# Merge gates moved to the front as seven half-size products a pair, and one fixed order of TensorE for the band, the linear attention and the second branch

## The chip, the cores and the metric

The kernel runs on one core of one Trainium2 chip. The metric is the device time of one launch in microseconds (us). Five engines work side by side: TensorE (PE, with its weight loads as PEld), VectorE (DVE), ScalarE (ACT), GpSimd (POOL) and SyncE (SP, which issues most DMAs). Each works through its own queue of instructions, and semaphores order the queues among one another.

## What is computed

One layer of a streaming encoder for 1056 tokens, 1024 of a prompt and 32 of a second request. In the reference, cut to what matters here:

```python
h = rms(x); z = h @ w_in   # -> GLA q,k,v,r,gate rank | band q,k,v | merge gates gA,gB
# branch A: gated linear recurrence, 4 heads
b = cumsum(log_a); scores = einsum(q_i, k_j, exp(b_i - b_j))   # causal
o = scores @ v + (q * exp(b)) @ S;  S = exp(b_last) * S + (k * exp(b_last - b))^T @ v
A = (rms(o) * g_gla * silu(r)) @ w_br_a
# branch B: softmax attention over a band of 64-frame chunks, 8 heads
B = band_attend(q, k, v, rel_bias) @ w_br_b
mix = (sigmoid(gA) * A + sigmoid(gB) * B) @ w_out;  x += rms(mix)
# then a ConvFFN and a per-layer embedding, which the change does not touch
```

The model width is 1024; gA and gB are 1024 columns each.

## The kernel before

Activations are kept transposed: features on the 128 partitions, the 1056 tokens along the free axis, in eight tiles of 128 features and three spans of 352 tokens (`CHUNKS`). A large product in fp32 accuracy is made of three matmuls for each block of 128x128 weights: high part of the weights by high part of the activations, high by low, low by high (`product`, L221 to L227). `weights` (L191) loads 512 KB of raw weights by a DMA on SP's queue, ACT rounds off the high part (`whi`, L204), POOL subtracts to get the low part (`wlo`, L205). `project` (L445) makes one tile of 128 columns of `w_in`: 8 blocks by 3 matmuls for each of 3 spans, 72 matmuls of 352 columns, and DVE takes each span out of PSUM with the factor 1/rms (L457).

The stages: a prologue (per-layer embedding product, split of x into `xh` and `xl`, the squares and the gate rank, L303 to L404), the band attention (four pairs of heads: scores, L541 and L542, DVE maximum L548, ACT exponential L550, transposes L557, product with v L599), the linear attention GLA (four heads), the second branch (band output times `w_br_b`, L987 to L1002), then branch A's product, `w_out`, the ConvFFN and the embedding. The merge gates (L634 to L642) are 16 calls of `project`, each with a sigmoid and a store to DRAM. They are emitted in portions after the pairs of the band and the heads of GLA (`BAND_GATES`, `GLA_GATES`), to be worked on between the attention's own steps.

A GLA head works in four segments of 256 tokens (the last has 288). For each, DVE and ACT build the decayed rows: differences `d` (L823), exponentials on ACT, products into the tile `x` (L826, L831), of which there are two buffers. PE makes scores from `x`, a diagonal (L851) and six levels (L859); DVE copies them into `scores` under masks (`copy_predicated`, L871, L875, L907); PE transposes one half of `scores` (L895) and multiplies by v and by the state (L917, L919). Once for each head stands the decay: three products by `wa` (L797), DVE L799, ACT exponential and logarithm, and DVE scans (L804).

The prologue and all that follows the second branch have their order written out by hand. The stages between are ordered by a scheduler when the kernel is built, from priorities and data dependences, engine by engine. What comes out is a fixed row of instructions for each engine, and each is worked through in that order.

## Time and profile before

| what | value |
|---|---|
| three runs | 1907.05, 1910.38, 1910.48 us; median 1910.38 |
| the profiled execution: span | 1907.2 us, 3.2 us under the median of the runs |
| TensorE busy | 1883.0 us in 13364 records |
| VectorE busy | 1263.1 us in 2533 |
| ScalarE busy | 908.4 us in 1674 |
| GpSimd busy | 464.8 us in 568 |
| prologue, band, GLA, second branch, rest | 0 to 44, 44 to 387, 387 to 880, 880 to 922, 922 to 1907 us |

A line of groups reads: line, engine, operation, output and inputs by the program's names, shape, count, then busy time and the mean duration in ns of one, then the time for which the engine stood idle ahead of them with what ended it. A line of windows reads: the stretch, its length, then for PE, PEld, DVE, ACT and POOL the busy us with the number of instructions, the granted clock of TensorE, the DMA share and GB/s. A busy TensorE says that its queue was never empty, not that each matmul had the shortest spacing; the spacing is the length of a window divided by its matmuls.

### The profile page before, as it was taken

Reading aid. Unit: us, or ns where it says so; the run is one execution under the profiler, and the core shown is the slowest. Engines: PE = TensorE matmul, PEld = TensorE weight load, DVE = VectorE, ACT = ScalarE, POOL = GpSimd, SP = SyncE. Lnnn points to the kernel's source line nnn. Section 1 sums busy time; section 2 is a strip of 40 time slices with the busy share of each in tenths; the row PEclk is TensorE's granted clock in tenths of the full one; section 3 lists DMA queues with packets and bytes.
Section 4 is the critical chain, followed back from the end, with each engine's and each line's share of the span. In section 5 each row is a group of like instructions: output and inputs, shape, how many; then the busy total and the mean of one; then the engine's idle time right before and its main releaser. Section 6 shows DMA issues by size and latency. Waiting matters only on the chain.

```text
span 1907.2 us, 34216 instructions
## 1 busy us (share of the span) xinstructions
PE 1883.0 (99%) x13364; PEld 1853.8 (97%) x13364; DVE 1263.1 (66%) x2533; ACT 908.4 (48%) x1674; POOL 464.8 (24%) x568
## 2 busy tenths in 40 slices
PE   9999999999999999999999999999999999999997
PEld 8999999999999999999999999999999999999997
DVE  6656556448487385675564787887777776556886
ACT  7456465434373352764334554434334344445554
POOL 2322222232222121221220113332222222115312
PEclk9999999999999999999999999999999999999999
DMA  7324346435344322227885356543433448556677
GB/s 275 121 98 131 109 126 166 108 123 152 100 139 128 110 73 80 92 92 265 313 281 184 108 171 224 188 168 124 158 128 128 144 150 298 190 187 195 216 262 148
DMA packets 107053, 307.77 MB, mean 161 GB/s; under 512 B 13252, under 2 KB 35724, under 8 KB 106764
## 3 DMA queue, kind: packets, MB, share of 16 engines
q1 hardware_dynamic: 80764, 217.64, 34.4%
q0 software_dynamic: 25296, 87.04, 15.5%
q8 instruction: 105, 1.72, 0.4%
q10 hardware_dynamic: 832, 0.90, 0.1%
q14 instruction: 56, 0.46, 0.1%
HBM read 217.79 MB, written 107.60 MB: 171 GB/s over the span
## 4 chain that ended last, share of the span: by engine, by line
PE 82%; DVE 10%; ACT 4%; issue 3%; DMA 1%; POOL 0%; SPq 0%; ACTq 0%; DVEq 0%; POOLq 0%
PE mm L225 13%; PE mm L226 13%; PE mm L227 13%; PE c L1748 11%; PE two L1484 6%; PE two L1486 6%; PE two L1485 6%; PE aux L1748 2%; PE one L599 2%; PE one L557 2%; PE two L859 1%; PE two L541 1%; PE one L917 1%; PE two L542 1%; DVE z L1854 1%
## 5 line engine op out<-in xcount | busy, mean ns | idle before, releaser
L225 PE MATMUL mm<-xh,whi 128*128 128x352 f32 (+2 forms) x1248 | 411.8, 330 | 0.0
L227 PE MATMUL mm<-xh,wlo 128*128 128x352 f32 (+2 forms) x1248 | 410.0, 329 | 0.0
L226 PE MATMUL mm<-xl,whi 128*128 128x352 f32 (+2 forms) x1248 | 408.6, 327 | 0.0
L205 POOL TENSOR_TENSOR wlo<-raw,whi 128x512 fp32r<-128x512 f32 x128 | 187.2, 1466 | 663.4 <-ACT whi L204 648.7
L225 PEld LDWEIGHTS mm<-xh,whi 128*128 128x128 f32 x1248 | 235.2, 188 | 2.1 <-DVE ev L457 0.7
L226 PEld LDWEIGHTS mm<-xl,whi 128*128 128x128 f32 x1248 | 235.0, 188 | 1.6 <-issue 0.7
L227 PEld LDWEIGHTS mm<-xh,wlo 128*128 128x128 f32 x1248 | 234.4, 188 | 0.9
L1486 PE MATMUL two<-mh,wlo 128*128 128x264 f32 x576 | 162.9, 284 | 0.0
L1485 PE MATMUL two<-ml,whi 128*128 128x264 f32 x576 | 162.5, 283 | 0.0
L1484 PE MATMUL two<-mh,whi 128*128 128x264 f32 x576 | 161.4, 284 | 0.4 <-ACT whi L230 0.4
L204 ACT ACTIVATE whi<-raw 128x512 fp32r<-128x512 f32 x136 | 84.1, 626 | 113.8 <-PE mm L226 84.1
L1748 PE MATMUL c<-mh,whi 128*128 128x264 f32 x396 | 112.4, 284 | 0.0
L1748 PE MATMUL c<-mh,wlo 128*128 128x264 f32 x396 | 112.3, 284 | 0.0
L1748 PE MATMUL c<-ml,whi 128*128 128x264 f32 x396 | 112.2, 283 | 0.0
L1485 PEld LDWEIGHTS two<-ml,whi 128*128 128x128 f32 x576 | 108.3, 188 | 0.0
L1486 PEld LDWEIGHTS two<-mh,wlo 128*128 128x128 f32 x576 | 108.3, 188 | 0.0
L1484 PEld LDWEIGHTS two<-mh,whi 128*128 128x128 f32 x576 | 107.3, 188 | 0.9 <-ACT whi L230 0.6
L457 DVE TENSOR_TENSOR ev<-mm,rstd 128x352 f32<-128x352 f32 x120 | 61.7, 518 | 60.4 <-PE mm L227 59.9
L1474 ACT ACTIVATE whi<-ws 128x512 fp32r<-128x512 f32 x72 | 45.5, 631 | 98.2 <-PE two L1485 63.6
L561 DVE TENSOR_TENSOR pt<-one,pt 128x128 fp32r<-128x128 f32 (+3 forms) x96 | 46.4, 499 | 51.4 <-ACT pt L560 51.2
L225 PE MATMUL mm<-mh,ahi 128*128 128x352 f32 x240 | 77.4, 322 | 0.0
L226 PE MATMUL mm<-ml,ahi 128*128 128x352 f32 x240 | 77.4, 322 | 0.0
(584 smaller groups left out, 5444.9 us busy)
## 6 DMA issues: line engine op xcount, KB each, us to landing
raw<-in_w_in SPq DMA_DIRECT2D x52, 512.0 KB, 3.8
uraw<-d_b POOLq DMA_DIRECT2D x33, 528.0 KB, 5.0
raw<-in_w_up SPq DMA_DIRECT2D x26, 512.0 KB, 3.6
d_b<-av POOLq DMA_DIRECT2D x44, 264.0 KB, 2.7
d_s<-in_w_down POOLq DMA_DIRECT2D x16, 704.0 KB, 8.3
draw<-d_s SPq DMA_DIRECT2D x16, 704.0 KB, 4.2
hn<-d_b POOLq DMA_DIRECT2D x40, 264.0 KB, 3.5
d_b<-hn POOLq DMA_DIRECT2D x40, 264.0 KB, 2.4
```

The lines of the kernel that those rows point to most:

```text
L204: ac.activation(hi[-1][:, d], raw[:, b], AF.Copy)
L205: eng.tensor_tensor(lo[-1][:, d], raw[:, b], hi[-1][:, d], op=ALU.subtract)
L225: pe.matmul(ps, h, xh(kt), start=(first and i == 0), stop=False)
L226: pe.matmul(ps, h, xl(kt), start=False, stop=False)
L227: pe.matmul(ps, l, xh(kt), start=False, stop=(last and i == n - 1))
L457: return lambda ps, s: ve.tensor_tensor(t[:, s], ps, rstd(s), op=ALU.mult)
L561: ve.tensor_tensor(out[1], tv, out[0], op=ALU.subtract)
L1474: ac.activation(h, x, AF.Copy)
L1484: pe.matmul(ps[:, j, :HC], w[0][:, k], x[0][:, k, s], start=st, stop=False, skip_group_check=True)
L1485: pe.matmul(ps[:, j, :HC], w[0][:, k], x[1][:, k, s], start=False, stop=False, skip_group_check=True)
L1486: pe.matmul(ps[:, j, :HC], w[1][:, k], x[0][:, k, s], start=False, stop=sp_, skip_group_check=True)
L1748: pe.matmul(ps, w, x, start=st, stop=sp_, skip_group_check=True)
```

## The change

It has four parts.

1. **Gates.** The 16 gate tiles are made in 8 pairs by a scheme of seven products in place of eight (`in_pair`, L566): the two column tiles, the two halves of the 1024 features and the two halves of the tokens form a 2x2 block product, DVE adds up sums of weights (`plus`, L573) and of activations (`t_scale` to `t_fourth`, L486 to L516), and each product (`mul`, L590) is 2 parts of 264 columns by 4 blocks by 3 matmuls, 24 matmuls. ACT rounds the high parts of the weights here and DVE makes the low parts (`weight`, L583). Sums of products are collected by DVE, POOL multiplies by 1/rms (`end`, L641), ACT does the sigmoid. All this stands between the prologue and the band, behind the three projections of the band's first pair.
2. **Prologue.** The sum over features for the first span (`x_total(0)`, L375) now follows the first of the three gate-rank products; it followed the third. The squares go to tiles of their own, since x is used again.
3. **Fixed order of TensorE** in band, GLA and second branch: `project` is a generator that gives three matmuls a step, and `fill(n)` puts n such steps between the steps of the attention, by the tables `BAND_FILL` and `GLA_FILL`. The projections of the next pair or head are the filling; in the last head's segments it is the second branch. DVE, ACT and POOL stay with the scheduler. The masked copies now all have high priority, and their emission precedes the rows of the following segment (`mid`, L1440), the decay of the next head (in each head's second segment) and its neighbours' factors (`gla_near`, in the third).
4. **Small ones.** The product with silu(r) leaves DVE in GLA (L947) for `row_load` in the second branch (L1374, POOL for tiles 0 to 5); q and k of head 0 are projected in the last pair of the band; in band and GLA the PSUM buffers of products (`mm`) go from three to two, those of the small matmuls (`one`) from three to four.

The core of the diff:

```diff
-PS_BAND = (3, 3, 1)
+PS_HEAD = (3, 3, 1)
+PS_BAND = (2, 4, 1)
+PS_GLA = (2, 4, 1)
+BAND_FILL = ((3, 2), (3, 2), (3, 2), (2, 1))
+GLA_FILL = ((7, 6, 6, 6), (8, 8, 8, 7), (8, 8, 8, 7), (6, 6, 6, 6))
...
     alr_product(0)
+    x_total(0)
     alr_out(0)
     alr_product(1)
+    x_inverse(0)
...
-            product(ps, hi, lo, [(k, k) for k in range(KT)], lambda k: xh[:, k, s], lambda k: xl[:, k, s])
+            for k in range(KT):
+                product(ps, hi, lo, [(k, k)], lambda k: xh[:, k, s], lambda k: xl[:, k, s], k == 0, k == KT - 1)
+                if k < KT - 1:
+                    yield
...
+        def mul(b, n, first, last):
+            if b not in ps:
+                ps[b] = bank()
+            x = XS[n]
+            for j in range(2):
+                s = slice(j * HC, (j + 1) * HC)
+                o = ps[b][0][:, j, :HC]
+                for k in range(HK):
+                    st_, sp_ = first and k == 0, last and k == HK - 1
+                    pe.matmul(o, w[n][0][:, k], x[0][:, k, s], start=st_, stop=False, skip_group_check=True)
+                    pe.matmul(o, w[n][0][:, k], x[1][:, k, s], start=False, stop=False, skip_group_check=True)
+                    pe.matmul(o, w[n][1][:, k], x[0][:, k, s], start=False, stop=sp_, skip_group_check=True)
...
+    repsum((0, 0, 4))
+    for i in range(7 * len(pairs_)):
+        if unit(i + LOOK):
+            unit(i + LOOK)[0]()
+        unit(i)[1]()
...
-    def gates(cnt):
-        for n, w0, dst in todo_gates[:cnt]:
-            g = evt()
-            project(w0 + n, to_tile(g))
-            ac.activation(g, g, AF.Sigmoid)
...
+            with tc.high_priority():
+                ve.copy_predicated(apart(pair, m), halves(masks[:, l], m), halves(place(l), m))
...
+        mid()
+        fill(F[0])
+        if before:
+            before()
+        kp = ps_one()
...
+        fill(F[1])
+        pe.transpose(kp[:, 256:384], pair[:, :P], ident)
...
+            def mid():
+                if i == 0 and h < 3:
+                    gla_load(h + 1)
+                if h == 0 and i in (0, 2):
+                    band_norm(2 + i // 2)
+                if i < 3:
+                    gla_rows(h, *SEGS[i + 1])
+                elif h < 3:
+                    gla_rows(h + 1, *SEGS[0])
+                if i == 1 and h < 3:
+                    gla_decay(h + 1)
+                if i == 2 and h < 3:
+                    while ("k", h + 1) not in ready:
+                        fill(1)
+                    gla_near(h + 1)
...
+        e.tensor_tensor(sr, l, sr, op=ALU.mult)
```

Three places of the order, as the built programs have it. First TensorE in the prologue. `accx` is the sum of squares, `was` the gate rank's weights, `mm` an accumulator in PSUM. Before, the third gate-rank product ends, and the total of the squares and the first projection follow:

```order
L384 MATMUL mm_467<-xh_133,was_154 48x352
L385 MATMUL mm_467<-xl_134,was_154 48x352
L250 MATMUL one_493<-accx_135,onesM_71 128x352
L225 MATMUL mm_573<-xh_133,whi_565 128x352
L226 MATMUL mm_573<-xl_134,whi_565 128x352
```

Of the changed kernel the same engine, where the first gate-rank product ends:

```order
L425 MATMUL mm_457<-xh_93,was_141 48x352
L426 MATMUL mm_457<-xl_94,was_141 48x352
L375 MATMUL one_474<-accx_145,onesM_71 128x352
L425 MATMUL mm_478<-xh_93,was_141 48x352
L426 MATMUL mm_478<-xl_94,was_141 48x352
```

The total (L250, now L375) has moved ahead of the second and third gate-rank products, 32 matmuls, which now queue behind it.

Second, TensorE in the second segment of GLA's head 0. Before, around its diagonals (L851) and levels (L859); `whi_5463`, `wlo_5468` and their like are weights of projections that the scheduler put between, `one_4770` is the norm of the segment ahead:

```order
L227 MATMUL mm_5497<-xh_133,wlo_5468 128x352
L225 MATMUL mm_5497<-xh_133,whi_5467 128x352
L246 MATMUL one_4770<-y_877_4771,onesHr_77 128x256
L851 MATMUL one_4837<-q_4053,k_4054 128x192 x2
L873 MATMUL one_4854<-ident_79,x_4789 128x128 x2
L859 MATMUL two_4956<-x_4906 128x128 x5
L247 MATMUL one_4770<-y_878_4772,onesHr_77 128x256
L859 MATMUL two_4956<-x_4906 128x128
L226 MATMUL mm_5497<-xl_134,whi_5467 128x352
```

Of the changed kernel, the same segment; L1239 and L1245 are the diagonals and levels, L1174 the decay products of head 1:

```order
L231 MATMUL mm_6860<-xh_93,whi_6852 128x352
L232 MATMUL mm_6860<-xl_94,whi_6852 128x352
L233 MATMUL mm_6860<-xh_93,wlo_6853 128x352
L1239 MATMUL one_6864<-q_6353,k_6354 128x192 x2
L1245 MATMUL two_6868<-x_6681 128x128 x6
L1174 MATMUL one_6934<-ev_6670,wa_1076_6672 128x352
L1174 MATMUL one_6938<-ev_6670,wa_1076_6672 128x352
L1174 MATMUL one_6942<-ev_6670,wa_1076_6672 128x352
```

Before, the levels that stand beside the second segment's diagonals are those of the third (`two_4956`); the second's own were made a segment earlier. Now each segment's diagonals and levels stand together, the next head's decay follows them, and then come 7 steps of projection, two matmuls of the norm, two transposes and 6 steps more, up to the transpose of `scores` (L1281).

Third, DVE at the same place. Before, the masked copies of the second segment (into `scores_784`) and the first rows of the third (into `x_4906`):

```order
L875 COPY_PREDICATED scores_783_4003<-eye_4047,one_4722 128x256
L907 COPY_PREDICATED scores_783_4003<-masks_4002,one_4722 128x64
L745 SCALAR_TENSOR_TENSOR q_5367<-mm_5407,rstd_84 128x3x128
L907 COPY_PREDICATED sct_4755<-masks_4002,one_4722 128x64
L871 COPY_PREDICATED scores_784_4004<-masks_4002,two_4839 128x32x2x2
L871 COPY_PREDICATED scores_784_4004<-masks_4002,two_4839 128x16x2x4
L871 COPY_PREDICATED scores_784_4004<-masks_4002,two_4839 128x8x2x8
L871 COPY_PREDICATED scores_784_4004<-masks_4002,two_4839 128x4x2x16
L871 COPY_PREDICATED scores_784_4004<-masks_4002,two_4839 128x2x2x32
L871 COPY_PREDICATED scores_784_4004<-masks_4002,two_4839 128x2x64
L826 TENSOR_TENSOR x_4906<-d_4907,k_4054 128x64x2
L831 TENSOR_TENSOR x_4906<-d_4907,q_4053 128x32x2 x2
```

Of the changed kernel, the last rows of the third segment (into `x_6883`), then the masked copies of the second (L1254) with differences `d`, the norm (`y_1130`) and the decay of head 1 (L1176, into `ev_6933`) between them:

```order
L1209 TENSOR_TENSOR x_6883<-d_6919,k_6354 128x2x64
L1214 TENSOR_TENSOR x_6883<-d_6919,q_6353 128x64 x2
L1254 COPY_PREDICATED scores_1028_6304<-masks_6302,two_6868 128x32x2x2
L250 TENSOR_TENSOR y_1130_6984<-sq_1104_6829,y_1129_6983 128x256
L1206 TENSOR_TENSOR d_7126<-b_6375 128x288
L1176 TENSOR_SCALAR ev_6933<-one_6934,vec_70 128x352
L1206 TENSOR_TENSOR d_7134<-b_6375 128x288
L1176 TENSOR_SCALAR ev_6933<-one_6938,vec_70 128x352
L1206 TENSOR_TENSOR d_7142<-b_6375 128x288
L1176 TENSOR_SCALAR ev_6933<-one_6942,vec_70 128x352
L1254 COPY_PREDICATED scores_1028_6304<-masks_6302,two_6868 128x16x2x4
```

The masked copies of a segment stood ahead of the rows of the segment after it; now they stand behind those rows and, here, the six copies are spread over 22 rows: the decay's differences, its nine scans (L1181), the neighbours' factors (L1193, L1195) and the norm (L261 to L263) come between them.

## The prediction

> **What bounds the kernel now.** I read the page's busy line first, then windows cut at the stages:

> ```profile
> PE 1883.0 (99%) x13364; PEld 1853.8 (97%) x13364; DVE 1263.1 (66%) x2533; ACT 908.4 (48%) x1674; POOL 464.8 (24%) x568
> ```

> ```profile
> 0.00:44.00 44.00, 40.17 (x211) 35.36 (x212) 27.41 (x39) 30.31 (x56) 10.17 (x15) 0.92 0.80 298
> 44.00:387.00 343.00, 340.65 (x2277) 329.38 (x2276) 192.21 (x438) 184.83 (x410) 94.26 (x94) 1.00 0.42 123
> 415.00:880.00 465.00, 462.31 (x3004) 453.38 (x3004) 314.93 (x957) 237.28 (x516) 108.18 (x74) 1.00 0.37 111
> 880.00:922.00 42.00, 42.00 (x260) 41.10 (x259) 19.97 (x43) 8.96 (x18) 9.38 (x7) 1.00 0.94 325
> 922.00:1907.00 985.00, 969.88 (x7438) 966.65 (x7436) 700.55 (x1038) 440.20 (x662) 231.24 (x346) 1.00 0.57 186
> ```

> TensorE is the bound in every stage up to 922 us, where the change ends; behind that nothing differs. In GLA (415 to 880) DVE is busy for 68%. The waits of TensorE, by what ended them, say how little the other engines cost there:

> ```profile
> PE two L541 <- DVE sm L548: 2.4, 4, 1.6
> PE two L859 <- DVE scores L871: 2.0, 3, 1.1
> PE mm L225 <- DVE ev L998: 0.4, 1, 0.4
> PE two L859 <- DVE x L831: 0.3, 1, 0.3
> ```

> So two questions decide: what TensorE is spared, and whether the new order makes it wait for DVE, which has less time to hide in once the gates are gone from GLA.

> **Spared work.** Two stretches of pure streams behind 922 us give the spacing of a matmul, with 352 columns in the first and 264 in the second:

> ```profile
> 1000.00:1050.00 50.00, 50.00 (x314) 50.00 (x313) 23.77 (x41) 20.02 (x36) 0.00 (x0) 1.00 0.53 186
> 1300.00:1350.00 50.00, 50.00 (x414) 50.00 (x413) 38.16 (x62) 18.51 (x26) 12.02 (x25) 1.00 0.39 132
> ```

> 50 us / 314 = 159.2 ns, 50 / 414 = 120.8 ns. Ahead of 922 us the streams are broken up by small matmuls; the groups of both kinds show it:

> ```profile
> L225 PE MATMUL mm<-xh,whi 128*128 128x352 f32 x1152 | 380.5, 330 | 0.0
> L225 PE MATMUL mm<-mh,ahi 128*128 128x352 f32 x240 | 77.4, 322 | 0.0
> ```

> The first is the interleaved stream, 330 ns against 322, and I charge it 7 ns more: 166 ns. Removed: 16 tiles x 72 = 1152 matmuls, 191.5 us (183.4 at 159.2). Added: 8 pairs x 7 products x 24 = 1344 matmuls of 264 columns, 162.4 us, and 1 us for their start. Term: **-28 us**, between -20 (no charge for interleaving) and -30.

> [...]

> **Front stage: is it hidden?** A pair takes TensorE 7 x 24 x 120.8 ns = 20.3 us. Beside it DVE has 16 instructions a pair, 512 or 528 wide (four sums of weights, seven low parts, five sums of products), ACT 11, POOL two products with 1/rms. For these I use the evacuation, 352 wide, and a POOL product 1056 wide with the DVE rows that met it:

> ```profile
> L457 DVE TENSOR_TENSOR ev<-mm,rstd 128x352 f32<-128x352 f32 x120 | 61.7, 518 | 60.4 <-PE mm L227 59.9
> 436.41 2.88 POOL L652 TENSOR_TENSOR ev<-ev,ev 128x1056 f32<-128x1056 f32 x1 [3.91 <-DMA ev<-d_inv]
> 437.59 1.99 DVE L823 TENSOR_TENSOR d<-b 128x256 f32<-128x256 f32 x1
> 442.61 0.41 DVE L823 TENSOR_TENSOR d<-b 128x256 f32<-128x256 f32 x1
> ```

> By width an instruction takes about 0.518 x 520 / 352 = 0.77 us, so DVE needs 12.2 us of 20.3. The same difference took 0.41 us alone and 1.99 while POOL's product ran (it ended at 439.29, and DVE's at 439.58). Two such blocks a pair, at most 2.9 us each, make 18 us: still inside 20.3. Term 0, bounds -1 to +8 (1 us a pair, should the four pairs of banks fill).

> [...]

> **Prologue.** The first gate-rank product is 16 matmuls, and the first span's sum of squares ends on DVE:

> ```profile
> 35.67 0.36 PE L384 MATMUL mm<-xh,was 128*48 128x352 f32 x1 [0.68 <-ACT ev L333]
> 38.11 0.32 PE L385 MATMUL mm<-xl,was 128*48 128x352 f32 x1
> 39.19 1.77 DVE L346 TENSOR_TENSOR accx<-accx,xin 128x352 f32<-128x352 f32 x3
> ```

> TensorE is through at 38.11 + 0.16 = 38.27, and the total now next in its queue needs 40.96: a wait of 2.7 us with the two other gate-rank products behind it. Before, these covered it. Nothing gives it back: **+2.7**, bounds 0 and 4.

> **Band.** Same products, same DVE work; DVE is busy for 192 of 343 us. Between two steps of a head stand 5 steps of filling, 15 matmuls or 2.4 us, against DVE's roughly 2 us of maximum, split and gather. The 2.4 us of L541 may go in part: **-1**, bounds -2 and +8.

> **Start of GLA.** Only the value products of head 0 (6 spans of 3.8 us) lie beside its decay, the casts of masks and the first rows, and two buffers must be emptied by DVE between them. In the list of instructions their evacuations stand behind decay steps. Cover for one evacuation is one span. **+3**, bounds 0 and 8.

> **GLA's segments.** This is the term that decides. A chain runs round once a segment: the rows of segment s+2 may start when TensorE's last product with segment s has freed one of the two `x` tiles; DVE works them off in its fixed order, and behind them come the masked copies of segment s+1, for which TensorE's transpose of `scores` (L1281) waits. Between the same two points TensorE has its filling. From the order I counted DVE's instructions and TensorE's records (a plain fp32 matmul has two) for the 15 turns:

> - DVE 61, 48, 40, 38; 55, 47, 39, 38; 62, 46, 39, 43; 52, 53, 10
> - TensorE 80, 77, 88, 92; 92, 89, 103, 89; 92, 89, 103, 77; 80, 74, 85

> The prices come from the stretches at the start of heads, where DVE does just such work and hardly stops, and from an undisturbed stretch for TensorE:

> ```profile
> 425.00:445.00 20.00, 18.66 (x114) 18.06 (x113) 19.90 (x70) 14.78 (x36) 5.59 (x3) 1.00 0.61 189
> 545.00:575.00 30.00, 29.77 (x193) 29.38 (x193) 27.25 (x98) 21.81 (x49) 9.78 (x5) 1.00 0.33 121
> 675.00:705.00 30.00, 30.00 (x197) 29.68 (x196) 27.02 (x101) 20.35 (x50) 9.43 (x6) 1.00 0.23 73
> 795.00:825.00 30.00, 29.35 (x190) 28.64 (x189) 27.54 (x101) 20.97 (x50) 9.99 (x4) 1.00 0.23 73
> 460.00:470.00 10.00, 10.00 (x68) 9.87 (x68) 7.88 (x19) 2.34 (x5) 3.44 (x3) 1.00 0.18 38
> ```

> DVE: 101.71 us / 370 = 0.275 us each, with POOL's interference in it. TensorE: 10 / 68 = 0.147. The first turn then is 61 x 0.275 = 16.8 against 80 x 0.147 = 11.8, a wait of 5.0. The turns with a surplus are 5.0, 1.9, 1.6, 3.5, 0.5, 2.5 and 3.7, together 18.7 us; a turn in which DVE is early banks nothing, since it stands before the freed `x`. Two 10 us stretches give the ends:

> ```profile
> 425.00:435.00 10.00, 9.73 (x64) 9.48 (x63) 9.97 (x41) 7.64 (x20) 1.26 (x1) 1.00 0.70 233
> 435.00:445.00 10.00, 8.93 (x52) 8.58 (x51) 9.93 (x31) 7.14 (x17) 4.32 (x2) 1.00 0.52 146
> ```

> At 9.97 / 41 = 0.243 the waits sum to 8 us, at 9.93 / 31 = 0.320 to 39. I take 18.7, since the four rows hold 370 instructions, less the 2.7 us of waits that the stage has now (2.0, 0.4 and 0.3 in the rows of waits above): **+16**, bounds +5 and +36.

> **End of the second branch.** The loads of the last two tiles of branch A's operand and of silu(r) queue on SP behind the store of the last product. One such load needs

> ```profile
> oa7l<-d_oa SPq DMA_DIRECT2D x1, 528.0 KB, 8.4
> ```

> and then a product on DVE; the first 68 matmuls of the next stage (10.8 us) do not need them. **+1**, bounds 0 and 4.

> **Sum.** -28 + 0 + 2.7 - 1 + 3 + 16 + 1 = -6.3 us. The profiled span, 1907.2, is 3.2 under the median; I apply the difference to the median: 1910.4 - 6.3 = **1904**. A measurement of this kernel can tell about 0.2% (3.8 us) from no change.

> **Rivals.**

> *Slower: DVE becomes the bound of GLA.* Place: the masked copies behind rows and decay, L1281 waiting. It decides where the price of a DVE instruction passes 0.29 us: there the waits are 25 us and the sum is nil. For it: 435 to 445 had 0.320, with POOL's 2.88 us product and a low-part split in it; two products with 1/rms (`band_norm`) still fall into head 0, and DVE waits on ACT's exponential and logarithm within the decay. Against it: 34 low-part splits on POOL remain in this stage (17 tiles, two each), where the row of the stage before had

> ```profile
> L205 POOL TENSOR_TENSOR wlo<-raw,whi 128x512 fp32r<-128x512 f32 x62 | 97.6, 1578 | 352.0 <-ACT whi L204 348.3 <-PE two L859 2.6 <-PE mm L227 1.0
> ```

> so there is less to collide with. At 0.320, and a start of GLA at +6: -28 + 2.7 - 1 + 6 + 36 + 1 = +17, **1927 us**. Chance 0.26.

> *Faster: the saving stays.* At 0.243 a DVE instruction the segments cost 8 - 2.7 = 5 and GLA's start nothing: -28 + 2.7 - 1 + 5 = -21, **1889**. The silu product gone from DVE (already out of my counts) and few splits on POOL speak for it; the first turns of heads, at 61 and 62 instructions, against. Chance 0.24.

> *Narrow matmuls are no cheaper here.* Were a matmul bound by the load of its weights, the seven products would cost 159.2 ns a matmul too: 1344 x 159.2 = 214 us against 191.5, +22.5 where I have -28, and 1904 + 51 = **1955**. The 120.8 ns of the 264-column stretch, same operand types and loads, speak against. Chance 0.03. [...]

> **How the numbers follow.** The forecast has 0.45, with 0.02 left for what I do not see. Around 1904 it spans 1897 to 1912, of which I count 0.29 as faster, 0.09 as the same, 0.07 as slower. The faster rival gives 0.22 to faster and 0.02 to same; the slower one 0.21 to slower, 0.05 to same; the third and the rest 0.04 to slower, 0.01 to same. Faster 0.51, same 0.17, slower 0.32. The range runs from 1886, the faster rival less the 3 us that the lower bounds of the gates' and the band's terms allow, to 1928, the slower rival.

> **What would show it.** Front stage: 1344 matmuls at 121 ns with TensorE never idle for over 1 us. Prologue: an idle time of 2 to 3 us before L375. GLA: idle time of TensorE before L1281, released by DVE's copies (L1257, L1265), 15 to 23 us in all, largest in the second segments of heads 0 and 2 and in the last head; nothing of the kind in the turns with 38 to 40 instructions. The forecast is wrong if those waits are under 8 us or over 30, if the front stage takes over 175 us, or if the band stalls on L548 for over 8.

## The result, and the profile after

The changed kernel took 1966.76 us in the median of four runs (1965.74 to 1966.93), the kernel before 1908.72 beside it: a ratio of 1.0309 with a 95% interval of 1.0294 to 1.0324. That is 58 us slower where I had forecast 6 us faster, and 39 us above the range.

The page's busy line of the changed kernel:

```profile
PE 1882.9 (96%) x13556; PEld 1850.5 (94%) x13556; DVE 1347.9 (69%) x2629; ACT 904.9 (46%) x1718; POOL 485.3 (25%) x555
```

TensorE is busy for as long as before (1883.0), though it was spared work, and the span grew by 1965.2 - 1907.2 = 58.0 us. What was spared must have been lost again in slower matmuls, and idle time came on top. Windows cut at the stages say where. The stages are prologue, the three projections, the gates, the first tile of r, the band, the start of GLA, GLA's segments with the second branch, and the rest:

```profile
0.00:48.00 48.00, 43.97 (x247) 38.88 (x248) 31.67 (x52) 34.71 (x69) 9.85 (x15) 1.00 0.78 293
48.00:84.00 36.00, 30.80 (x186) 30.04 (x185) 28.34 (x39) 17.99 (x27) 13.41 (x10) 0.99 0.19 66
84.00:262.00 178.00, 171.97 (x1359) 171.34 (x1359) 118.34 (x143) 67.02 (x104) 47.34 (x21) 0.96 0.32 107
262.00:278.00 16.00, 9.52 (x59) 9.23 (x57) 7.58 (x8) 11.39 (x16) 10.57 (x14) 0.89 0.68 209
278.00:566.00 288.00, 278.10 (x1881) 270.90 (x1882) 170.49 (x404) 164.10 (x375) 66.44 (x61) 0.98 0.42 118
566.00:609.00 43.00, 38.65 (x241) 37.23 (x240) 27.96 (x94) 18.62 (x56) 23.80 (x46) 1.00 0.51 144
609.00:980.00 371.00, 339.82 (x2163) 326.32 (x2164) 264.77 (x854) 152.91 (x415) 81.92 (x45) 0.96 0.41 129
980.00:1965.00 985.00, 970.04 (x7430) 966.59 (x7428) 698.74 (x1039) 438.14 (x661) 231.98 (x346) 0.99 0.57 188
```

Length less busy time of TensorE is 4.0, 5.2, 6.0, 6.5, 9.9, 4.4 and 31.2 us in the seven stages up to 980, 67 us together; the kernel before had 922 us with 9 us idle in the same part of the work. Branch A and all behind it take 985 us in both. What ended the long waits, as line waited for, total, times and longest:

```profile
PE one L1281 <- DVE scores L1257: 19.4, 5, 7.2
PE one L953 <- DVE pt L914: 7.3, 3, 3.1
PE two L897 <- DMA kh<-kh: 6.7, 1, 6.7
PE two L599 <- DVE ev L475: 4.4, 1, 4.4
PE one L1319 <- DMA state<-in_state_gla: 3.9, 1, 3.9
PE two L599 <- ACT xs L652: 2.9, 1, 2.9
```

Here L1281 is the transpose of `scores`, L953 the product with v in the band, L897 the band's scores, L599 the first matmul of a gate product and L1319 the product with the GLA state. Only the first row was a term of my sum. And idle time is not all: the granted clock was 0.996 over the span before and is 0.982 now, and in three of the stages above it is 0.96 or lower. The timeline of TensorE around the longest wait in GLA shows what that means:

```profile
636.75 0.32 PE L233 MATMUL mm<-xh,wlo 128*128 128x352 f32 x1
644.27 0.45 PE L1281 MATMUL one<-ident,scores 128*128 128x128 f32 x1 [7.20 <-DVE scores L1257]
...
648.28 0.50 PE L232 MATMUL mm<-xl,whi 128*128 128x352 f32 x1
648.57 0.49 PE L233 MATMUL mm<-xh,wlo 128*128 128x352 f32 x1
...
650.39 0.33 PE L231 MATMUL mm<-xh,whi 128*128 128x352 f32 x1
650.56 0.32 PE L232 MATMUL mm<-xl,whi 128*128 128x352 f32 x1
```

Behind the wait the starts are 0.29 us apart in place of 0.16 until 650.2, six microseconds after the wait ended. I counted such matmuls ahead of branch A (start to start over 1.55 times the median of their kind, no idle time between): 173 with 18.4 us of excess before, 253 with 31.8 us now. The granted clock says it more plainly. Around this wait it was half:

```profile
639.87:650.10 10.23, 5.83 (x19) 5.50 (x20) 6.34 (x15) 0.49 (x2) 1.33 (x1) 0.50 0.21 80
```

Ahead of branch A there are eleven such stretches, 58.0 us in all, and TensorE was busy in 48.3 of them; before there was one, of 6.8 us near the kernel's start. The matmuls that start in them take some 22 us more than the median of their kind at full clock, against 3 before, so 19 us more (an estimate from the two traces).

### The profile page after: what moved, and what is told of

The parts are those of the page before. It is cut to its first block, busy times and chain, and to the rows that moved or that the text cites. A ratio compares the mean times of both kernels' runs of the same rounds, so it can differ in the third digit from the quotient of the medians.

```text
span 1965.2 us, 34770 instructions
## 1 busy us (share of the span) xinstructions
PE 1882.9 (96%) x13556; PEld 1850.5 (94%) x13556; DVE 1347.9 (69%) x2629; ACT 904.9 (46%) x1718; POOL 485.3 (25%) x555
## 3 DMA queue, kind: packets, MB, share of 16 engines
q10 hardware_dynamic: 1024, 1.28, 0.2%
## 4 chain that ended last, share of the span: by engine, by line
PE 72%; DVE 15%; ACT 6%; issue 3%; DMA 3%; POOL 1%; SPq 0%; DVEq 0%; ACTq 0%; POOLq 0%
PE c L2209 9%; PE mm L231 9%; PE mm L232 9%; PE mm L233 9%; PE two L1945 6%; PE two L1947 6%; PE two L1946 6%; PE two L599 2%; PE two L600 2%; PE two L601 2%; PE aux L2209 2%; PE one L953 2%; PE one L911 1%; DVE z L1598 1%; PE two L897 1%
## 5 line engine op out<-in xcount | busy, mean ns | idle before, releaser
L231 PE MATMUL mm<-xh,whi 128*128 128x352 f32 (+2 forms) x864 | 296.9, 344 | 2.8 <-DVE ev L475 2.8
L233 PE MATMUL mm<-xh,wlo 128*128 128x352 f32 (+2 forms) x864 | 282.1, 327 | 0.0
L232 PE MATMUL mm<-xl,whi 128*128 128x352 f32 (+2 forms) x864 | 281.5, 326 | 0.0
L211 POOL TENSOR_TENSOR wlo<-raw,whi 128x512 fp32r<-128x512 f32 x88 | 138.0, 1572 | 429.0 <-ACT whi L210 417.5
L231 PEld LDWEIGHTS mm<-xh,whi 128*128 128x128 f32 x864 | 165.6, 192 | 6.4 <-DVE ev L475 3.5
L232 PEld LDWEIGHTS mm<-xl,whi 128*128 128x128 f32 x864 | 165.3, 191 | 1.0
L233 PEld LDWEIGHTS mm<-xh,wlo 128*128 128x128 f32 x864 | 164.1, 190 | 0.0
L210 ACT ACTIVATE whi<-raw 128x512 fp32r<-128x512 f32 x104 | 64.6, 626 | 76.1 <-PE mm L232 64.2
L599 PE MATMUL two<-xh,whi 128*128 128x264 f32 x256 | 76.1, 297 | 10.5 <-DVE ev L475 4.4
L904 ACT ACTIVATE s<-s,sm 128x640 f32<-128x640 f32 (+5 forms) x72 | 50.4, 700 | 68.4 <-DVE sm L903 66.6
L914 DVE TENSOR_TENSOR pt<-one,pt 128x128 fp32r<-128x128 f32 (+3 forms) x96 | 45.7, 499 | 48.3 <-ACT pt L913 48.0
L231 PE MATMUL mm<-mh,ahi 128*128 128x352 f32 x240 | 77.5, 323 | 0.0
## 6 DMA issues: line engine op xcount, KB each, us to landing
uraw<-d_b POOLq DMA_DIRECT2D x33, 528.0 KB, 5.0
```

The lines of the kernel that those rows point to most:

```text
L210: ac.activation(hi[-1][:, d], raw[:, b], AF.Copy)
L211: eng.tensor_tensor(lo[-1][:, d], raw[:, b], hi[-1][:, d], op=ALU.subtract)
L231: pe.matmul(ps, h, xh(kt), start=(first and i == 0), stop=False)
L232: pe.matmul(ps, h, xl(kt), start=False, stop=False)
L233: pe.matmul(ps, l, xh(kt), start=False, stop=(last and i == n - 1))
L599: pe.matmul(o, w[n][0][:, k], x[0][:, k, s], start=st_, stop=False, skip_group_check=True)
```

## The experiments

Theory 1: the loss is a sum of waits of TensorE at fixed places of its new order, in each of which another engine's queue holds what TensorE needs behind other work, and slow clock behind the longer waits. The main rival: DVE has too little time as a whole once the gates no longer stand in GLA, so that any order loses about as much. Times are compared by their ratio to the kernel before, which ran beside each (1905.9 to 1908.7 us).

### TensorE's order left to the scheduler

```diff
-    order = tc.manual_schedule(engines={mybir.EngineType.PE})
+    order = contextlib.nullcontext()
     order.__enter__()
     fillers.append(gla_rest(rests.pop(0)))
```

> The changed kernel with TensorE in band, GLA and second branch left to the scheduler again; the gates stay in front with their seven products, and the filling steps remain as emission order. Theory 1 (the loss is waits of TensorE at fixed places of the new order, and slow clock behind them): the waits at the starts of band pairs and before the transposes of scores, about 27 us with some 16 us of slow clock, go for the most part, while the front's 9 us and the keys' 6.7 us stay; about 1920 us. Rival (DVE and ACT have too little time in GLA without the gates as filling, whatever TensorE's order): above 1950 us, with the waits elsewhere.

It took 1942.16 us, ratio 1.0188 (1.0173 to 1.0203), against 1.0309: 23 us of the 58 belong to the order written out by hand. It was less than I expected. In GLA the wait before the transpose of `scores` fell from 19.4 us to 0.7, but the products of the norm (L252) now wait twice, once for 6.3 us:

```profile
PE one L252 <- ACT y L249: 10.5, 2, 6.3
...
PE one L1281 <- DVE scores L1257: 0.7, 1, 0.7
```

### The clock kept open in six waits

```diff
+        for i in range(WARM_TURN.get((h, t0 // 256), 0)):
+            pe.matmul(kp[:, 384:512], onesM, onesM, start=True, stop=True)
         pe.transpose(kp[:, 256:384], pair[:, :P], ident)
```

> The changed kernel with small matmuls on constants put ahead of six waits (20 before the first scores of the band, 24, 12, 10 and 10 before four transposes of scores, 12 before the last chunk's products); no wait is taken away, the filling is shorter than each wait. Theory 1 with the clock: behind each of these waits some 13 matmuls ran at 0.22 to 0.29 us in place of 0.12 to 0.16; with the gate kept open the time falls by 8 to 10 us to about 1957, and the spacing behind the waits is 0.16 at once. Rival (the slow spacing behind a wait comes from the work there, not from the idle time): no change, 1966 +/- 2.

1960.17 us, ratio 1.0281 (1.0258 to 1.0304): about 5 us by the ratios, whose intervals overlap, and less than expected. The trace is plainer than the time. At the same wait as above:

```profile
641.21 5.52 PE L1285 MATMUL one<-onesM 128*128 128x128 f32 x48
648.49 0.33 PE L1286 MATMUL one<-ident,scores 128*128 128x128 f32 x1 [1.75 <-DVE scores L1260]
...
649.68 0.32 PE L233 MATMUL mm<-xl,whi 128*128 128x352 f32 x1
649.84 0.32 PE L234 MATMUL mm<-xh,wlo 128*128 128x352 f32 x1
```

The wait is as long as it was (the filling's 5.52 us and 1.75 idle against 7.20), and the spacing behind it is 0.16 at once. From the transpose to the first product with v went 6.6 us before (644.27 to 650.88) and 3.9 now. The excess that I counted ahead of branch A fell from 31.8 us to 24.7, and the time at half clock from 58.0 us to 41.0. So the slow spacing behind this wait came from TensorE's idleness, not from the work behind it, and the wait cost some 2.7 us more than its own length.

The granted clock goes with the spacing: it is 0.50 in the row 639.87:650.10 above, where the spacing is 1.8 times as long for some 6 us behind the wait of 7.2, and the eleven stretches at half clock last 3.4, 6.8 or 10.2 us. That the length of a wait alone does not decide it is told in the last section.

### DVE's order in GLA written out, masked copies first

```diff
+    order = tc.manual_schedule(engines={mybir.EngineType.PE, mybir.EngineType.DVE})
...
-        mid()
-        fill(F[0])
+        rows_left = mid()
+        next(rows_left, None)
+        fill(F[0] // 2)
+        next(rows_left, None)
+        fill(F[0] - F[0] // 2)
         if before:
             before()
```

> The changed kernel with DVE's order in GLA written out as well: masked copies right behind their levels, the rows of the next segment behind them in portions, the scans of the decay late in the segment. Theory 1: the 19.4 us before the transpose of scores go and with them about 8 us of slow clock; about 1940 us. Rival (DVE has too little time): the waits move to the evacuation of products or to the levels, and the time stays within 8 us of 1966.

2053.65 us, ratio 1.0779 (1.0763 to 1.0795), a miss for both sides of the expectation. The wait before the transposes was gone, and this stood in its place:

```profile
PE one L253 <- DVE y L250: 55.8, 15, 9.1
```

In my order the low part for the norm (L250) came behind the rows, and TensorE needs it a little after the first filling. One late instruction in a queue of fixed order cost more than the 19.4 us that the order was to save; the run does not tell whether a good order of DVE exists.

### Two tiles of r ahead of the band, the state loaded early

```diff
     fillers.append(gla_rest(rests.pop(0)))
+    fillers.append(gla_rest(rests.pop(0)))
     band_keys(0, 0)
...
-                state = tl(gp, [P, 256], tag="state", bufs=4)
-                dma.dma_start(state, a["state_gla"][h])
+                state = state8
```

> The changed kernel with two tiles of r in place of one between the gates and the band (taken from the last pair's filling), and the second request's state loaded at the start of the last segment in place of its end. Theory 1: the 6.7 us before the band's first scores and the 3.9 us before the last chunk go, with some 4 us of slow clock; about 1952 us. Rival (the cover is only moved, and the last pair, with less filling, gives the time back): 1962 to 1968.

1959.76 us, ratio 1.0279 (1.0264 to 1.0295): 6 us less by the ratios, whose intervals touch, and less than half of what I expected. Both waits went (no row of L897 on `kh`, none of L1319 on the state), but products waited for evacuations instead, at the same place for 4.0 us: the keys' splits stand ahead of the evacuations on DVE.

### The same filling by turns

```diff
-GLA_FILL = ((7, 6, 6, 6), (8, 8, 8, 7), (8, 8, 8, 7), (6, 6, 6, 6))
+GLA_FILL = (((4, 4, 6, 6), (18, 17, 6, 6), (8, 8, 6, 6), (7, 6, 6, 6)),
+            ((5, 4, 8, 7), (10, 11, 8, 7), (8, 8, 8, 7), (8, 8, 8, 7)),
+            ((4, 4, 8, 7), (14, 14, 8, 7), (7, 6, 8, 7), (8, 8, 8, 7)),
+            ((6, 6, 6, 6), (10, 10, 6, 6), (10, 10, 6, 6), (6, 6, 6, 6)))
```

> The changed kernel with the same filling put elsewhere: the steps of projection between GLA's steps are set turn by turn (37 in place of 19 in the second segment of head 0, 27 for 23 and 35 for 23 in those of heads 1 and 2, 26 for 18 in the second branch's two heavy turns; fewer in the turns where the copies are early), and one tile of r goes from the last pair of the band to head 0. No work of DVE changes. Theory 1 (a wait is the surplus of DVE's time over TensorE's in one turn, so filling placed there removes it): the 19.4 us before the transposes fall under 5, with 6 us of slow clock: about 1943. Rival (DVE as a whole has too little time in GLA): the waits reappear in the turns that lost filling, 1960 or more.

1957.60 us, ratio 1.0275 (1.0251 to 1.0300): 6 us, with intervals that overlap, between the two expectations. The longest waits of GLA and the second branch are now these; the wait of the transposes was 19.4 us (L1281), products waited for 2.4 us (L231) and the transposes of v for 3.1 in all (L1155):

```profile
PE mm L234 <- DVE ev L1417: 9.6, 5, 3.3
PE one L1158 <- ACT vt L1159: 5.5, 8, 0.7
PE one L1284 <- DVE scores L1260: 4.3, 3, 2.5
```

The 15 us before the transposes (L1281, now L1284) went as the theory has it. About half came back, since TensorE's idle time from GLA's first segment to branch A fell only from 31.1 us to 23.4: in head 3 products of the second branch waited for DVE's evacuations (L1417), and the transposes of v, left without products between them, for ACT's copies (L1158).

### The front: low parts later, products ahead of weights

```diff
+        if eng is ve:
+            low_parts()
+            held.append((l, src, h))
...
-        if unit(i + LOOK):
-            unit(i + LOOK)[0]()
         unit(i)[1]()
+        if unit(i + LOOK):
+            unit(i + LOOK)[0]()
```

> The changed kernel with two things in the front turned: the low parts of the activations' sums are taken one step later on DVE, so that it does not wait for ACT's rounding each time, and a product of the gates with its evacuation stands ahead of the weights for the product after next. Theory 1 (the front's 9.3 us of waits come from DVE and ACT handing each of twelve low parts to and fro while the three projections cover them): the waits before the first products fall to 3 or less, with 3 us of slow clock: about 1957. Rival (DVE's work is too long for the cover, order or not): 1964 to 1967.

1991.88 us, ratio 1.0437 (1.0419 to 1.0455): two changes in one run, and the second cost far more than the first gained. The first wait of 4.4 us fell to 0.7, but products in the pairs now waited for their weights, which come a product later:

```profile
PE two L609 <- ACT whi L596: 18.8, 10, 3.0
PE two L611 <- DVE wlo L597: 3.1, 8, 1.6
...
PE two L609 <- DVE ev L475: 0.7, 1, 0.7
```

In the later runs only the first was kept.

### GLA without its norm

The squares, their sum, the inverse root and the scaling of GLA's output are left out.

```diff
-            inv_rms(rs, acc, "H", gp, 1, split=NS_GLA, cw=288)
-            for j in range(2):
-                o = ot[:, j, :nt]
-                ve.scalar_tensor_tensor(o, o, col(G_GLA + 2 * h + j), rs, op0=ALU.mult, op1=ALU.mult)
```

> The changed kernel without the norm of GLA's output (squares, sum, inverse root, scaling are left out), which takes six DVE instructions and some 3.8 us of DVE, and two matmuls of TensorE, out of each turn. Theory 1 (DVE's time in a turn sets the wait): the waits of 7.2, 1.5, 4.2, 3.2 and 3.3 us before the transposes fall by 3.8 each, to about 4 in all, with 6 us of slow clock and 5 us of matmuls: about 1940. Rival (ACT's exponentials or the order set those waits): they stay at 15 us or more and the time at 1955 or more.

1936.99 us, ratio 1.0161 (1.0146 to 1.0176), as theory 1 had it.

```profile
PE one L1281 <- DVE scores L1257: 4.9, 3, 3.3
```

The waits before the transposes fell from 7.2, 1.5, 4.2, 0.4, 3.2 and 3.3 us to 3.3, 0, 0, 1.1, 0 and 0.5: in the first turn by 3.9. There DVE's time from the first row (L1209) to the copy that the transpose waits for (L1257) fell from 20.2 us to 15.2: the norm's instructions had taken 3.7 of it, and one instruction (L1193), 2.18 us long beside a POOL product, took 0.16 us in this run. Three waits went to nothing, one fell by 2.8, and one rose by 0.7. So DVE's time between the freed `x` and the masked copies sets this wait.

### More filling at each change of pair

```diff
                     late[0][-1][1]()
-                    fill(F[0])
+                    fill(F[0] + 7)
                     late[0][-2][2]()
```

> The changed kernel with seven more steps of projection ahead of the product with v that follows each change of pair in the band. Theory 1: the 7.3 us of waits there (DVE takes the low parts of the next head's keys first) fall under 2, with 4 us of slow clock: about 1957. Rival (the steps are missing at the end of the pair): 1964 to 1968.

1961.43 us, ratio 1.0284 (1.0262 to 1.0305), some 5 us, with intervals that touch. In the band the waits for `pt` fell from 7.3 us to 1.1; the one for the first keys, which the edit does not touch, was longer in this run (9.8 for 6.7):

```profile
PE two L897 <- DMA kh<-kh: 9.8, 1, 9.8
...
PE one L953 <- DVE pt L914: 1.1, 2, 0.8
```

### All remedies, with the fixed order and with the scheduler

The low parts later, two tiles of r, the state early and more filling at the pairs; in the first kernel also filling by turns (a milder table), in the second the scheduler in place of the fixed order.

> The changed kernel with the remedies together: the low parts of the front one step later (without the swap of product and weights), two tiles of r ahead of the band, seven steps more at each change of pair, filling set turn by turn in GLA (32, 32, 39 steps in the heavy second segments), the state loaded early. Theory 1 (waits at places, each with its slow clock): of 66 us of idle time before branch A's product some 45 go, and 12 of slow clock: about 1910, level with the kernel before. Rival (DVE as a whole too short of time in GLA and second branch): half of it comes back elsewhere, 1930 or more.

> The same remedies (without the filling by turns) with TensorE's order from the band on left to the scheduler, which alone gave 1942. Theory 1: the front's 9.3 us and its slow clock go and the early state helps; about 1928. Rival (the scheduler's order already took what was to be had): 1938 to 1944.

1951.14 us, ratio 1.0237 (1.0222 to 1.0252), and 1925.42, ratio 1.0109 (1.0092 to 1.0126). With the fixed order the rival's forecast held (1930 or more): only a quarter of the loss came off, and 11.2 us before the transposes were left (four waits, the longest 4.5). With the scheduler it was 15 us less, by the ratios, than with the scheduler alone, a little better than expected: from GLA's first segment to branch A TensorE is idle for 9 us of 340. In this stretch DVE is busy for 276.7 us, 81%, so that DVE has too little time as a whole is not what happened.

```profile
599.00:939.00 340.00, 330.90 (x2165) 321.54 (x2164) 276.70 (x874) 159.90 (x432) 70.45 (x45) 0.98 0.45 144
0.00:939.00 939.00, 904.27 (x6157) 876.54 (x6158) 662.83 (x1596) 471.33 (x1066) 242.53 (x210) 0.99 0.44 136
```

Of the 35 us idle ahead of branch A some 26 now lie ahead of GLA.

### One more step in the front, and half of the gates back in GLA

The first kernel is the scheduled one above with the gates' first product moved ahead of the third's weights, and PSUM as `(3, 3, 1)`. The second is this one again, with gate B's eight tiles as plain projections among the filling of heads 0 to 2 and a longer `GLA_FILL`:

```diff
-    pairs_ = [(w0 + n, w0 + n + 1, (d[n], d[n + 1])) for w0, d in ((GA0, d_ga), (GB0, d_gb)) for n in range(0, 8, 2)]
+    pairs_ = [(w0 + n, w0 + n + 1, (d[n], d[n + 1])) for w0, d in ((GA0, d_ga),) for n in range(0, 8, 2)]
```

> The scheduled kernel with the remedies (1925), and two more: the first product of the gates with its copy out of PSUM stands ahead of the weight sums for the third product, and three PSUM buffers for products in place of two from the band on. Theory 1: the 4.9 us wait in the front (ACT's copy queued behind a rounding that waits for DVE's sums) and its slow clock go, and the 4.3 us of waits for evacuations shrink: about 1916. Rival (the waits only move): 1921 to 1927.

> The same, but only the eight tiles of gate A are made in front by seven products; the eight of gate B go back into GLA as plain projections between its steps (heads 0 to 2). TensorE has 14 us more work by this. Theory 1 (the gates were the cover for DVE's work in GLA): idle time of TensorE from the first segment of GLA to branch A's product falls by 8 us or more, and the time is within 6 us of the run beside it. Rival (the waits there do not depend on the cover): idle as beside, and the time 12 to 16 us longer.

1943.64 us, ratio 1.0192 (1.0175 to 1.0209), and 1937.46, ratio 1.0157 (1.0142 to 1.0172). The first is a loss of 16 us, by the ratios, on the scheduled kernel with the remedies. The 4.9 us wait in the front was gone, but TensorE was idle for 22.7 us in GLA, where its longest waits are now for copies out of the small matmuls' PSUM, which has one buffer fewer (the two edits were not run apart):

```profile
PE one L1299 <- ACT kt L1292: 7.0, 2, 4.3
PE one L1305 <- ACT kt L1292: 3.3, 1, 3.3
PE one L1305 <- DVE sct L1302: 3.1, 1, 3.1
```

With half of the gates back, the same stretch of the two kernels:

```profile
598.00:954.00 356.00, 333.32 (x2129) 319.75 (x2128) 278.09 (x879) 160.33 (x433) 77.44 (x46) 0.96 0.44 137
```

```profile
516.00:948.00 432.00, 421.00 (x2719) 411.92 (x2718) 293.20 (x902) 201.18 (x472) 97.95 (x62) 0.98 0.42 134
```

Idle time is 11.0 us in place of 22.7, at 590 more matmuls in the stretch and some 11 us more work in all (1152 / 2 matmuls of 159.2 ns for 1344 / 2 of 120.2), and the time is 6 us shorter. So here gates in GLA hide more than the work that they add. This is shown for PSUM as `(3, 3, 1)` alone: with `(2, 4, 1)` the stretch had 9 us idle without any gates in it, and that kernel, at 1925.42, is faster than this one.

None of these kernels beats the one before. The nearest, the scheduled one with the remedies, stays 1.1% above it.

## Why the prediction was wrong

**The terms side by side.** Measured is the idle time of each stage less that of the kernel before, in us, by the windows of the two kernels (from 387 to 415 us the kernel before was never idle); the two estimates are worked out below.

| term | forecast | measured |
|---|---|---|
| TensorE's work spared | -28 | -19 (estimate) |
| prologue | +2.7 | +0.2 |
| front stage: three projections and gates | 0 | +11.2 |
| band, with the tile of r ahead of it | -1 | +14.0 |
| start of GLA | +3 | +4.4 |
| GLA's segments and second branch | +16 and +1 | +28.5 |
| slow clock | no term | +19 (estimate) |

**What held.** The waits before the transposes in GLA's segments: I had 18.7 us, in seven turns of 5.0, 1.9, 1.6, 3.5, 0.5, 2.5 and 3.7; the trace has 19.9 in the same turns, 7.2, 0.1, 1.5, 4.2, 0.4, 3.2 and 3.3. The sum is nearer than its parts, which miss by up to 2.2 us either way, so some of it is luck; in the first turn one DVE instruction of 16 columns (L1193) took 2.18 us beside a POOL product of 2.74, and 0.16 us in the run without the norm. Where DVE's time in that turn fell by 5.0 us, its wait fell by 3.9. What the term left out are the other waits of the stage: TensorE is idle there for 31.2 us, not 19.9, with 3.9 for the state and 2.4 and 1.5 for exponentials and the norm as the longest of the rest. The start of GLA (+3) measured 4.4. The narrow products came at 25 us / 208 = 120.2 ns:

```profile
125.00:150.00 25.00, 25.00 (x208) 25.00 (x207) 17.16 (x22) 10.07 (x16) 6.23 (x3) 1.00 0.44 152
```

and the prologue's total waited for 1.2 us in all where I had 2.7.

**The front stage, "Term 0, bounds -1 to +8".** This step failed at the start. The sign that I had named, over 175 us, came: the stretch of the gates took 178. I priced DVE's work per pair and never the operand sums ahead of the first one: the low parts (eight on DVE, four on POOL) and the sums under them, which DVE and ACT hand to and fro. DVE was busy for 28.3 of the 36 us of the three projections, and its idle time came mostly in turns of 0.7 us, each waiting for ACT's rounding. Its evacuation of the last projection stood behind all that: 4.4 us, then 2.9 and 2.0 until the queue had caught up. And of the four sums of L498, DVE operations with both inputs in SBUF, the two that began while POOL was at work took 2.63 and 1.85 us, the two others 0.70 and 0.69:

```profile
63.65 1.85 DVE L498 TENSOR_TENSOR xs<-xs 128x528 f32<-128x528 f32 x1
68.47 0.70 DVE L498 TENSOR_TENSOR xs<-xs 128x528 f32<-128x528 f32 x1
63.61 1.32 POOL L490 TENSOR_TENSOR t3l<-xs,t3h 128x528 fp32r<-128x528 f32 x1 [4.28 <-ACT t3h L489]
```

Behind that the pairs were hidden but for 1.2 us, as I had it. With the low parts one step later the 4.4 us fell to 0.7.

**The band, "-1, bounds -2 and +8".** It lost 7.5 us within the band (idle 9.9 against 2.4 before) and 6.5 just ahead of it. My cover was right for the steps within a head (2.2 us of waits at L911, all under a microsecond) and did not ask what stands in DVE's queue at a change of pair: the low parts of the next head's keys, 1.3 and 2.7 us long, ahead of what L953 waits for:

```profile
345.95 1.26 DVE L881 TENSOR_TENSOR kl<-ev,kh 64x1056 fp32r<-64x1056 f32 x1
347.79 2.67 DVE L881 TENSOR_TENSOR kl<-kc,kh 64x512 fp32r<-64x512 f32 x1
```

And that the keys of the first pair are split on ACT behind the last gates' sigmoids, which wait for POOL (ACT was idle for 6.06 us ahead of L645), was not looked at. Seven more steps of filling took 6 us off the first. A second tile of r took away the second, of which 4.0 us came back as waits for evacuations.

**The end of the second branch, "+1".** Nothing waits there; but 3.9 us are lost in the last segment, where SP's queue brings the state late. The early load removed it.

**The sum had no term for the clock.** I let a wait cost its own length. A stretch at half clock costs some 2 us, and there are eleven: 19 us by the granted clock, 13.4 us by my count, beyond the kernel before. Where six waits were filled, 7 us of the count went, though the filling takes no wait away.

**The saving, "-28 us".** Too large. By the spacing of pure streams it is 1152 x 159.2 - 1344 x 120.2 = 21.9 us; by the medians of all kinds of matmul ahead of branch A 19.1. The 7 ns that I charged to interleaving did not come back; I take it, without a run that shows it, that the products that remain are interleaved as before.

The balance ahead of branch A: -19.1 of work, +58.3 of idle time (67.2 less 8.9, by the windows) and +13.4 of slow matmuls by my count make +52.6 of 58.0. With the 19 us of the granted clock in place of the count it closes, but no better than to some 5 us, since the work spared comes out between 18 and 25 us by how the kinds of matmul are grouped. The rival that I had for the slow side (a price of 0.320 us for each of DVE's instructions) is not what happened: at the price that I had, the waits before the transposes came out right in sum. The loss lies in the places that had no term, each small, in the clock, and in a saving that was too large. What TensorE's fixed order cost is 23 us, shown by the first experiment. With the remedies on top, 38 of the 58 us came off. Another 9 us of idle time ahead of GLA and 6 within it came off with the remedies under the scheduler (49 to 34 us ahead of branch A). What remains is 4.9 us at one gate product, seventeen waits of 0.7 to 2.5 us, and shorter ones; which of them the last 1.1% is made of was not shown.

Open is whether a fixed order of TensorE could be had that waits less: by the ratios the filling by turns gained 6 us and all remedies together 14, while DVE's order lost 90. A wait that was removed turned up, in part, at the next instruction that needed the same queue, in at least four of the twelve kernels (the first, third, fourth and fifth).

## What to carry to other kernels

When the engine that sets the time gets a fixed order and its cover is taken away, list every instruction at which it can wait, not only the tightest loop: the first use of each stage's operands, each change of pair or head, each load on a shared queue; ask for each what stands ahead of the releaser in its own queue. Work that looks like a candidate for a cheaper form may be what hides another engine's work: price it with the waits that it covers. And a wait of TensorE may cost more than it lasts: look at the granted clock behind it. Here eleven stretches at half clock added about a third to the 58 us of idle time.

## What the runs showed of the hardware

```profile
87.85 0.28 PE L600 MATMUL two<-xl,whi 128*128 128x264 f32 x1
87.97 0.28 PE L601 MATMUL two<-xh,wlo 128*128 128x264 f32 x1
91.13 0.59 PE L599 MATMUL two<-xh,whi 128*128 128x264 f32 x1 [2.87 <-ACT xs L652]
91.51 0.42 PE L600 MATMUL two<-xl,whi 128*128 128x264 f32 x1
91.73 0.42 PE L601 MATMUL two<-xh,wlo 128*128 128x264 f32 x1
```

The length of the wait does not decide alone. Behind one of 2.00 us (110.74) the spacing was 0.22 for 264 columns, and behind one of 1.48 us (858.65) 0.29 for 352. Behind one of 2.42 us (903.66) it was 0.16, and so it was behind this one of 3.28 us:

```profile
931.43 0.30 PE L1281 MATMUL one<-ident,scores 128*128 128x128 f32 x1 [3.28 <-DVE scores L1257]
...
932.59 0.32 PE L232 MATMUL mm<-q,whi 128*128 128x352 f32 x1
932.75 0.32 PE L233 MATMUL mm<-vt,wlo 128*128 128x352 f32 x1
```

What else decides was not tested.

A DVE sum of two inputs in SBUF (L498) took 1.85 us beside POOL's 1.32 us subtraction (L490) and 0.70 alone.
